# A hybrid S5/SSD layer on one core: strips without an order edge, S5 output blocks among the gate tiles, SSD chain started two tiles later

## The chip, the cores and the metric

The kernel runs on one core of a Trainium2 chip. The metric is the device time of one execution in microseconds (us). It is the median of several runs; the profile comes from one further execution. The core has five engines that work side by side: TensorE (PE, matmuls), VectorE (DVE), ScalarE (ACT), GpSimd (POOL) and SyncE (SP, which here only issues DMAs). Each engine works through its own queue in order.

## The reference

One layer with two parallel branches over 1024 frames of width 1024, in float32, cut to what matters here:

```python
hn   = rmsnorm(h, norm_w)
u_s5, z_s5, z_ssd, xBC, dt_raw = split(hn @ w_in)
y_s5  = s5_branch(u_s5, ...)        # 64 groups of 16 channels, 64 complex states each
y_s5  = y_s5 * sigmoid(y_s5 @ w_glu + b_glu) * silu(z_s5)
y_ssd = gated_group_rmsnorm(ssd(silu(conv(xBC)), dt) + D * x, z_ssd)
h = h + concat(y_s5, y_ssd) @ w_out
h = h + (p @ w_ple) * sigmoid(rmsnorm(h) @ w_gate)
return rmsnorm(h, final_norm_w)
```

The S5 branch is a linear recurrence per channel group, the SSD branch a chunked scan with 16 heads; both are causal in time.

## The kernel before, in words

**Dense tiles.** All large products are "dense tiles": 48 matmuls of 128x128 by 128x512 (8 steps over the contraction, 2 halves of the frames, and 3 products, since each float32 operand is split into a high and a low part, `hi` and `lo`). `wload` (L125 to L135) loads one weight tile on SP, makes `whi` on ACT (L131) and `wlo` on VectorE or, from the 29th tile on, on POOL (L134). The dense tiles in order: 8 tiles for the S5 input `u`; 20 tiles in the order of `SEQ`, 16 conv tiles (`conv_tile`, "c") and 4 gate tiles (`z_tile`, "z"); a second loop with the other 12 gate tiles; 8 GLU tiles; 8 tiles of the first half of the output projection (operand `m`); 8 of its second half (operand `n`, made from the SSD's result); then the gate of the last stage.

**Work between the tiles.** The S5 and SSD branches are Python generators, `s5_chain` and `ssd_chain`. Between (or in the middle of) dense tiles the program calls `pull(gen, n)`, which writes the next `n` steps of the chain into the program. `PU`, `PX`, `PZ`, `PG` and `PO` hold how many steps go beside each tile: `PU` beside the u tiles, `PX` beside the 20 tiles of `SEQ`, `PZ`, `PG`, `PO` for the SSD chain beside the second gate loop, the GLU tiles and the output projection (each twice per tile: in its middle and behind it).

**Who sets the order.** The program is built with `schedule_with_timeline_sim=True`: the builder keeps an estimate of every instruction's time and writes each engine's queue in the order in which instructions become ready by that estimate. Of those that are ready, the one that stands earlier in the program goes first. `in_line` (L191 to L195) adds an order edge without a wait: the second instruction is put into its queue only after the first has been put into its own.

**S5.** `s5_weights` (from L320) works on eight blocks b. For each it loads `br` and `gr`, forms two products (L365, L366) and sums (L368) for `wx`, and forms `CA` from six VectorE operations (L378 to L383). `strips` (L341) then makes a small matrix `Ks` of the block before: 8 matmuls on PE (L345; 16 records), two drains on VectorE (L351, L352) and a store on SP (`Kd`, L353). Each strip matmul has an order edge to the current block's L366. When all blocks are done their memory goes to the next pools. `s5_states` loads `ug` (L396) and makes states (L420), then scans along time on VectorE and ACT. `s5_out` writes eight output blocks: for each, loads of `CAr` (L462), eight of `tp` (L465) and one of `ug`, 16 matmuls (L479, L480), a gelu on ACT (L482) and a store `Yd` (L483). Two blocks' buffers exist at a time; the loads of block b+1 are written ahead of block b's matmuls. After the last block the S5 memory is free; the SSD chain's pool lies in the same place.

**SSD.** `ssd_chain` has a first load step and four steps for each of eight chunks, 33 in all. Step one of a chunk: 16 operations on the decay tile `csB` (L593), its exponential on ACT (L597), score matmuls (L600), products (L602), transposes (L609) and scaled copies `xd` (L613). Step two: loads of the next chunk (`cc` L575, `csB` L578), the output matmuls (L625, L633) and sums (L627, L636, L637). Steps three and four: gate, group norm (L655 to L658), state update (L667, L672) and the store `Sd` (L659). After the chain, `m2raw` (L873) reads the eight `Sd` tiles back through two buffers, ACT scales them (L875) and L218, L219 split them into `nhi` and `nlo`, the operand of the output projection's second half.

**The second gate loop.** It runs over the 12 gate tiles left; behind tile 5 (index 4) and later ones it loads one tile of `m` from `Yd` (L828).

Of the kernel before, what the change touches and what calls it, by code (L numbers as in the profile page):

```python
# [11 lines left out]
ALU = mybir.AluOpType  # L12

P = 128
# [13 lines left out]

PU = [0, 1, 2, 2, 2, 1, 2, 1]
SEQ = "cczzccccccccczzccccc"  # L30
PX = [3, 3, 1, 1, 2, 1, 2, 1, 0, 2, 1, 2, 2, 0, 1, 1, 2, 2, 2, 2]


PZ = [0, 0, 0, 0, 0, 1, 1, 1, 1, 1, 1, 1]
PG = [1, 1, 1, 1, 1, 1, 1, 1]
PO = [1, 1, 1, 0, 0, 0, 0, 0]
NZ = SEQ.count("z")

ZORD = list(range(8, 16)) + list(range(8))
# [16 lines left out]
def hybrid_layer(ctx: ExitStack, tc: tile.TileContext, xT, pT, w_in, w_dt, w_glu, w_out, w_gate, w_ple,  # L56
                 prm, cst, bst, cstt, brow, out):
    nc = tc.nc
    V, S, G, T = nc.vector, nc.scalar, nc.gpsimd, nc.tensor
# [13 lines left out]
    def pr(n, i=None, w=1):  # L73
        a, b = po[n]
        return prm_t[:, a:b] if i is None else prm_t[:, a + i:a + i + w]

    def cs_(n):
        a, b = co[n]
        return cst_t[:, a:b]
# [27 lines left out]
    def psa():  # L107
        return ps_a.tile([P, 512], F32, tag="a", name="psa")
# [33 lines left out]
    def wnext(ahead=1):  # L142
        wfetch(1)
        w = wq.pop(0)
        wfetch(ahead)
        return w
# [43 lines left out]
    def in_line(ins):  # L190

        for a, b in zip(ins, ins[1:]):
            tc.add_manual_dep(b.ins, a.ins.name, mybir.DependencyInfo(mybir.DependencyClass.NoSync, mybir.DependencyReason.DATA),
                              reason="in line")

    def evac(ps, dst, func=AF.Copy):
        for h in range(2):
            S.activation(hf(dst, h), ps[h], func)
# [24 lines left out]
    def pull(gen, n=1):  # L223
        for _ in range(n):
            if next(gen, "end") == "end":
                return False
        return True
# [90 lines left out]
    def s5_weights(Er, Ei, qr, qi, wx):  # L318

        fl = lambda t: t.rearrange("p a b c -> p (a b c)")  # L320
        with ExitStack() as es:
            qb = es.enter_context(tc.tile_pool(name="qb", bufs=1, side="right"))
            Bbd = qb.tile([P, 2, 32, 32], F32, tag="Bbd", name="Bbd")
            G.memset(Bbd, 0.0)
            with tc.tile_pool(name="qt", bufs=1, side="right") as q2:
                bs = q2.tile([P, 2, 32, 16], F32, tag="bs", name="bs")
                dma(bs.rearrange("p a b c -> p (a b c)"), bst)

                bt1 = q2.tile([P, 32, 16], F32, tag="bt1", name="bt1")
                bt2 = q2.tile([P, 32, 16], F32, tag="bt2", name="bt2")  # L330
                for ri, (x, y, op) in enumerate(((qr, qi, ALU.subtract), (qi, qr, ALU.add))):
                    V.tensor_tensor(bt1, bs[:, 0], x[:, :, None].broadcast_to([P, 32, 16]), ALU.mult)
                    V.tensor_tensor(bt2, bs[:, 1], y[:, :, None].broadcast_to([P, 32, 16]), ALU.mult)
                    for g2 in range(2):
                        r = slice(64 * g2, 64 * g2 + 64)
                        V.tensor_tensor(Bbd[r, ri, :, 16 * g2:16 * g2 + 16], bt1[r], bt2[r], op)
                yield
            q2 = es.enter_context(tc.tile_pool(name="q2", bufs=2, side="right"))
            csb = q2.tile([P, 2, 32, 16], F32, tag="csb", name="csb", bufs=1)
            dma(csb.rearrange("p a b c -> p (a b c)"), cstt)  # L340
            def strips(b, CA, behind):  # L341
                kp = psa()
                for q in range(4):
                    for ri in range(2):
                        i_ = T.matmul(kp[32 * q:32 * q + 32, 0:P], Bbd[:, ri, 4 * b + q, :],  # L345
                                      CA[:, ri, q, 0:8, :].rearrange("p a b -> p (a b)"),
                                      start=(ri == 0), stop=(ri == 1), tile_position=(0, 32 * q))
                        in_line((behind, i_))
                Ks = q2.tile([P, 240], F32, tag="Ks", name="Ks", bufs=1)
                G.memset(Ks[:, 0:112], 0.0)  # L350
                V.scalar_tensor_tensor(Ks[:, 112:128], cs_("diag"), pr("s5D", b), kp[:, 0:16], ALU.mult, ALU.add)  # L351
                V.tensor_copy(Ks[:, 128:240], kp[:, 16:P])  # L352
                dma(Kd[b], Ks)  # L353

            for b in range(8):
                br = q2.tile([P, 2, 512], F32, tag="br", name="br", bufs=1)
                gr = q2.tile([P, 2, 512], F32, tag="gr", name="gr")
                w1 = q2.tile([P, 2, 512], F32, tag="w1", name="w1", bufs=1)
                dma(br, brow[:, :, b * 512:(b + 1) * 512].rearrange("r p c -> p r c"))

                src = Gd.rearrange("s (b g) c -> s b (g c)", b=8)[:, b]
                dma(gr.rearrange("p r c -> p (r c)"), src[:, None, :].broadcast_to([8, 16, 1024]))
                wi = wx[:, 8 * b:8 * b + 8]
                g8 = lambda ap: ap.rearrange("p (g c) -> p g c", g=8)
                V.tensor_tensor(wi, br.rearrange("p r (g c) -> p g r c", g=8), g8(gr[:, 0])[:, :, None, :].broadcast_to([P, 8, 2, 64]), ALU.mult)  # L365
                behind = V.tensor_tensor(w1, br, gr[:, 1:2].broadcast_to([P, 2, 512]), ALU.mult)  # L366
                for r, op in ((0, ALU.subtract), (1, ALU.add)):
                    V.tensor_tensor(wi[:, :, r], wi[:, :, r], g8(w1[:, 1 - r]), op)  # L368
                CA = q2.tile([P, 2, 4, 9, 16], F32, tag="CA", name="CA")
                ca1 = q2.tile([P, 4, 9, 16], F32, tag="ca1", name="ca1", bufs=1)  # L370
                ca2 = q2.tile([P, 4, 9, 16], F32, tag="ca2", name="ca2", bufs=1)
                g4 = slice(4 * b, 4 * b + 4)
                sh = [P, 4, 9, 16]
                cr = csb[:, 0, g4, None, :].broadcast_to(sh)
                ci = csb[:, 1, g4, None, :].broadcast_to(sh)
                er = Er[:, J0:J0 + 9, g4].rearrange("p j g -> p g j")[:, :, :, None].broadcast_to(sh)
                ei = Ei[:, J0:J0 + 9, g4].rearrange("p j g -> p g j")[:, :, :, None].broadcast_to(sh)
                V.tensor_tensor(ca1, cr, er, ALU.mult)  # L378
                V.tensor_tensor(ca2, ci, ei, ALU.mult)
                V.tensor_tensor(fl(CA[:, 0]), fl(ca1), fl(ca2), ALU.subtract)  # L380
                V.tensor_tensor(ca1, cr, ei, ALU.mult)
                V.tensor_tensor(ca2, ci, er, ALU.mult)
                V.scalar_tensor_tensor(fl(CA[:, 1]), fl(ca1), -1.0, fl(ca2), ALU.mult, ALU.subtract)  # L383
                for g2 in range(2):
                    dma(CAd[b, g2].rearrange("r n c -> n r c"),
                        CA[64 * g2:64 * g2 + 64].rearrange("p a b c d -> p a (b c d)"))
                if b > 0:
                    strips(b - 1, last, behind)
                last = CA
                yield  # L390
            strips(7, last, behind)
            yield

    def load_u(pool, b):
# [284 lines left out]
    s5 = s5_chain()  # L679
# [110 lines left out]
    def z_tile(m, mid=None):  # L790

        z = pz.tile([P, NT], F32, tag="z", name="z")
        ps = dense(wnext(), xhl, mid=mid)
        if m < 8:
            evac(ps, z, AF.Silu)
        else:
            zk = z.rearrange("p (k t c) -> p t k c", k=8, t=8)
            for h in range(2):
                S.activation(zk[:, 4 * h:4 * h + 4], ps[h].rearrange("p (t k c) -> p t k c", t=4, k=8), AF.Silu)
        dma(Zd[m], z)  # L800
# [4 lines left out]
    with tc.tile_pool(name="p3", bufs=2) as p3:  # L805
        at = {"c": 0, "z": 0}
        for c, n in zip(SEQ, PX):
            m = at[c]
# [3 lines left out]
            else:  # L812
                z_tile(ZORD[m])
            pull(s5, n)
    while pull(s5):
        pass


    es_m = ExitStack()
# [2 lines left out]
    ssd = ssd_chain()  # L822
    for m, n in zip(range(NZ, 16), PZ):
        z_tile(ZORD[m], lambda: pull(ssd, n))

        for i in range(8)[m - NZ - 4:m - NZ - 3] if m >= NZ + 4 else ():
            for h2 in range(2):
                dma(mt[i][64 * h2:64 * h2 + 64].rearrange("p (t c) -> p t c", t=8), Yd[:, :, 2 * i + h2, :])  # L828
        pull(ssd, n)
# [19 lines left out]
    for m in range(8):  # L849
        dma(h_t[m], xT[m])  # L850
        ps = dense(wnext(), mhl, mid=lambda: pull(ssd, PO[m]))
        for h in range(2):
            V.tensor_tensor(hf(h_t[m], h), hf(h_t[m], h), ps[h], ALU.add)
        pull(ssd, PO[m])
    while pull(ssd):
# [46 lines left out]
    for cols in ((slice(0, 384), slice(384, 768)), (slice(768, NT),)):  # L902
        end = cols[-1].stop == NT
        for m in range(8):
            pp = dense(wnext(3), phl, nk=2, cols=cols, bank=psa)
            pg = dense(wnext(3), hhl, cols=cols)
            for i, c in enumerate(cols):
# [3 lines left out]
                last = S.activation(gt, gt, AF.Sigmoid)  # L911
# [129 lines left out]
```

## Time and profile before

| | us |
|---|---|
| median of 3 runs | 1009.69 |
| lowest and highest of them | 1008.46, 1011.22 |
| the profiled execution | 1010.22 |
| its span, first to last instruction | 1008.4 |
| PE busy in the span | 964.2 |
| VectorE busy | 614.2 |
| ACT busy | 462.6 |
| POOL busy | 245.5 |

The profiled execution took 1.8 us more than its span. Matmuls overlap their neighbours in the records, so PE's busy time says when PE had work, not that it was at its peak. The view of waits gives the idle time of an engine with the instruction that ended it. In the views of time, "[6.93 <-DVE CA L383]" behind an instruction says that its engine had stood idle for 6.93 us, until an instruction of VectorE at line 383 that writes CA. PEclk is the granted share of the full TensorE clock.

### The profile page before, as it was taken

Reading aid. Unit: us, or ns where it says so; the run is one execution under the profiler, and the core shown is the slowest. Engines: PE = TensorE matmul, PEld = TensorE weight load, DVE = VectorE, ACT = ScalarE, POOL = GpSimd, SP = SyncE. Lnnn points to the kernel's source line nnn. Section 1 sums busy time; section 2 is a strip of 40 time slices with the busy share of each in tenths; the row PEclk is TensorE's granted clock in tenths of the full one; section 3 lists DMA queues with packets and bytes.
Section 4 is the critical chain, followed back from the end, with each engine's and each line's share of the span. In section 5 each row is a group of like instructions: output and inputs, shape, how many; then the busy total and the mean of one; then the engine's idle time right before and its main releaser. Section 6 shows DMA issues by size and latency. Waiting matters only on the chain. (4 is left out here: it accounts for less than half of the span.)

```text
span 1008.4 us, 13149 instructions
## 1 busy us (share of the span) xinstructions
PE 964.2 (96%) x4992; PEld 809.6 (80%) x4992; DVE 614.2 (61%) x972; ACT 462.6 (46%) x605; POOL 245.5 (24%) x166
## 2 busy tenths in 40 slices
PE   8999979997999999899989999899999999999994
PEld 5778857787888888788778888787888888899994
DVE  7599689953988994000666968679511511444677
ACT  8444122363855544224456754547233522453373
POOL 0000000000000043001134345444332363332353
PEclk9999979998999999999999999999999999999998
DMA  7135778578423136997996868556354330011233
GB/s 296 40 86 142 206 222 270 163 186 208 133 97 105 63 104 192 253 264 210 248 322 175 229 188 230 161 153 188 121 172 145 133 128 21 1 58 53 70 134 115
DMA packets 136270, 158.56 MB, mean 157 GB/s; under 512 B 6288, under 2 KB 108688, under 8 KB 135184
## 3 DMA queue, kind: packets, MB, share of 16 engines
q1 hardware_dynamic: 136208, 157.74, 53.3%
q8 instruction: 39, 0.64, 0.3%
q14 instruction: 23, 0.19, 0.1%
HBM read 118.06 MB, written 39.65 MB: 156 GB/s over the span
## 5 line engine op out<-in xcount | busy, mean ns | idle before, releaser
L134 POOL TENSOR_TENSOR wlo<-wraw,whi 128x1024 fp32r<-128x1024 f32 x52 | 140.2, 2698 | 272.6 <-ACT whi L131 260.5
L131 ACT ACTIVATE whi<-wraw 128x1024 fp32r<-128x1024 f32 x79 | 83.3, 1056 | 241.8 <-PE psd L155 205.2
L155 PE MATMUL psd<-xnlo,whi 128*128 128x512 f32 x592 | 186.2, 394 | 0.2 <-DVE xnlo L766 0.2
L155 PE MATMUL psd<-xnhi,whi 128*128 128x512 f32 x592 | 185.1, 393 | 0.0
L155 PE MATMUL psd<-xnhi,wlo 128*128 128x512 f32 x592 | 184.7, 393 | 0.1
L155 PEld LDWEIGHTS psd<-xnlo,whi 128*128 128x128 f32 x592 | 110.8, 189 | 25.0 <-issue 1.6
L155 PEld LDWEIGHTS psd<-xnhi,wlo 128*128 128x128 f32 x592 | 111.0, 189 | 24.3 <-issue 1.0
L155 PEld LDWEIGHTS psd<-xnhi,whi 128*128 128x128 f32 x592 | 111.0, 189 | 23.1 <-issue 0.4
L593 DVE SCALAR_TENSOR_TENSOR csB<-csB,csM,cst_t 128x128 f32<-128x128 f32 x128 | 45.3, 427 | 101.6 <-DMA m<-Yd 93.5
L566 DVE SCALAR_TENSOR_TENSOR cv<-pad,prm_t,cv 128x1024 f32<-128x1024 f32 x48 | 65.8, 1371 | 11.9 <-ACT cv L564 11.7
L557 POOL MEMSET pad<- 128x3 f32 x16 | 1.6, 104 | 217.1 <-DMA Cd<-pad 186.0
L155 PE MATMUL psd<-hhi,whi 128*128 128x384 f32 (+1 forms) x192 | 50.7, 318 | 0.5 <-DVE gt L910 0.5
L155 PE MATMUL psd<-hlo,whi 128*128 128x384 f32 (+1 forms) x192 | 50.8, 317 | 0.0
L155 PE MATMUL psd<-hhi,wlo 128*128 128x384 f32 (+1 forms) x192 | 50.7, 318 | 0.0
L884 DVE TENSOR_TENSOR h<-h,psd 128x512 f32<-128x512 f32 x16 | 10.4, 683 | 63.3 <-PE psd L155 63.3
L134 DVE TENSOR_TENSOR wlo<-wraw,whi 128x1024 fp32r<-128x1024 f32 x27 | 32.9, 1220 | 15.9 <-ACT whi L131 8.1
L155 PE MATMUL psd<-yhi,whi 128*128 128x512 f32 x128 | 41.0, 398 | 0.0
L155 PE MATMUL psd<-yhi,wlo 128*128 128x512 f32 x128 | 40.7, 395 | 0.0
L155 PE MATMUL psd<-mhi,wlo 128*128 128x512 f32 x128 | 40.1, 391 | 0.0
L155 PE MATMUL psd<-ylo,whi 128*128 128x512 f32 x128 | 40.0, 391 | 0.0
L155 PE MATMUL psd<-mlo,whi 128*128 128x512 f32 x128 | 39.5, 390 | 0.0
L155 PE MATMUL psd<-nhi,wlo 128*128 128x512 f32 x128 | 39.4, 389 | 0.0
(292 smaller groups left out, 1896.1 us busy)
## 6 DMA issues: line engine op xcount, KB each, us to landing
wraw<-in_w_in_dram SPq DMA_DIRECT2D x39, 512.0 KB, 3.8
Cd<-pad SPq DMA_DIRECT2D x16, 512.0 KB, 2.8
Zd<-z SPq DMA_DIRECT2D x16, 512.0 KB, 3.8
ug<-Ud SPq DMA_DIRECT2D x16, 512.0 KB, 6.1
cc<-Cd SPq DMA_DIRECT2D x8, 1024.0 KB, 9.8
csB<-Rd SPq DMA_DIRECT2D x8, 1024.0 KB
wraw<-in_w_out_dram SPq DMA_DIRECT2D x16, 512.0 KB, 5.1
wraw<-in_w_gate_dram SPq DMA_DIRECT2D x16, 512.0 KB, 3.5
```

What stands on the lines that cost most here:

```text
L131: S.activation(hi, raw, AF.Copy)
L134: E.tensor_tensor(lo, raw, f(hi), ALU.subtract)
L155: T.matmul(p, w[:, c], rhs[k][r][:, x], start=(k == 0 and j == 0), stop=(k == nk - 1 and j == 2))
L557: G.memset(pad[:, 8:11, 0:1], 0.0)
L566: conv_last[0] = V.scalar_tensor_tensor(cv, pad[:, d:d + 8, 1:129], pr("convw", 4 * m + d), cv, ALU.mult, ALU.add)
L593: i_ = V.scalar_tensor_tensor(csB[:, h], csB[:, h], csM[:, 16 * k + h:16 * k + h + 1], cap, ALU.subtract, ALU.min)
L884: V.tensor_tensor(hf(h_t[m], h), hf(h_t[m], h), ps[h], ALU.add)
```

## The change

Three things are edited. The strips lose their order edge to L366. `PX` is changed: the first entries from 3, 3, 1 to 1, 4, 2, the last five from 1, 2, 2, 2, 2 to 0, 1, 0, 1, 0; it now holds 24 steps, so that the last five output blocks are left over, and the new list `PS` writes one of them behind each of the first five tiles of the second gate loop, the chain's end behind the fifth. `PZ` starts two tiles later; `PO` goes on for two tiles more, so that the SSD chain has as many pulls as before.

```diff
-PX = [3, 3, 1, 1, 2, 1, 2, 1, 0, 2, 1, 2, 2, 0, 1, 1, 2, 2, 2, 2]
-PZ = [0, 0, 0, 0, 0, 1, 1, 1, 1, 1, 1, 1]
+PX = [1, 4, 2, 1, 2, 1, 2, 1, 0, 2, 1, 2, 2, 0, 1, 0, 1, 0, 1, 0]
+PS = [1, 1, 1, 1, 1]
+PZ = [0, 0, 0, 0, 0, 0, 0, 1, 1, 1, 1, 1]
 PG = [1, 1, 1, 1, 1, 1, 1, 1]
-PO = [1, 1, 1, 0, 0, 0, 0, 0]
+PO = [1, 1, 1, 1, 1, 0, 0, 0]
...
-            def strips(b, CA, behind):
+            def strips(b, CA):
                 kp = psa()
                 for q in range(4):
                     for ri in range(2):
-                        i_ = T.matmul(kp[32 * q:32 * q + 32, 0:P], Bbd[:, ri, 4 * b + q, :],
-                                      CA[:, ri, q, 0:8, :].rearrange("p a b -> p (a b)"),
-                                      start=(ri == 0), stop=(ri == 1), tile_position=(0, 32 * q))
-                        in_line((behind, i_))
+                        T.matmul(kp[32 * q:32 * q + 32, 0:P], Bbd[:, ri, 4 * b + q, :],
+                                 CA[:, ri, q, 0:8, :].rearrange("p a b -> p (a b)"),
+                                 start=(ri == 0), stop=(ri == 1), tile_position=(0, 32 * q))
...
-                behind = V.tensor_tensor(w1, br, gr[:, 1:2].broadcast_to([P, 2, 512]), ALU.mult)
+                V.tensor_tensor(w1, br, gr[:, 1:2].broadcast_to([P, 2, 512]), ALU.mult)
...
-                    strips(b - 1, last, behind)
+                    strips(b - 1, last)
...
-            strips(7, last, behind)
+            strips(7, last)
...
-    while pull(s5):
-        pass
...
     for m, n in zip(range(NZ, 16), PZ):
         z_tile(ZORD[m], lambda: pull(ssd, n))
+        if m - NZ < len(PS):
+            pull(s5, PS[m - NZ])
+        if m - NZ == len(PS) - 1:
+            while pull(s5):
+                pass
```

## Rows read from the trace of the kernel before

**Rows 1.** The page's head: span, and busy time of each engine.

```profile
span 1008.4 us, 13149 instructions
...
PE 964.2 (96%) x4992; PEld 809.6 (80%) x4992; DVE 614.2 (61%) x972; ACT 462.6 (46%) x605; POOL 245.5 (24%) x166
```

**Rows 2.** Waits of PE: releaser, us in total, times, longest.

```profile
PE psa L345 <- DVE CA L383: 6.9, 1, 6.9
PE psa L420 <- DMA ug<-Ud: 5.3, 1, 5.3
PE psa L479 <- DMA tp<-Kd: 4.8, 3, 2.1
PE psa L625 <- DVE xd L613: 3.5, 2, 3.2
...
PE psa L170 <- DVE nl L168: 1.5, 2, 1.1
...
PE psa L625 <- DVE csB L602: 1.4, 1, 1.4
...
PE psa L609 <- DVE st L672: 1.2, 1, 1.2
```

**Rows 3.** PE in order of time, 130 to 160 us: start, us, instruction.

```profile
142.42 1.10 PE L345 MATMUL psa<-CA,Bbd 128*32 128x128 f32 x14 [6.93 <-DVE CA L383]
```

**Rows 4.** Windows behind four waits: us, busy by engine, PEclk, DMA, GB/s.

```profile
142.40:148.40 6.00, 5.98 (x26) 4.58 (x27) 6.00 (x9) 0.00 (x0) 0.00 (x0) 0.53 1.00 277
237.60:244.00 6.40, 6.38 (x31) 6.40 (x32) 2.44 (x2) 2.88 (x4) 0.13 (x2) 0.53 0.51 154
437.60:442.90 5.30, 5.17 (x32) 5.20 (x33) 0.00 (x0) 0.60 (x1) 0.00 (x0) 0.68 1.01 314
522.50:527.50 5.00, 4.94 (x42) 4.37 (x43) 4.86 (x15) 1.86 (x1) 0.18 (x1) 0.66 1.08 367
```

**Rows 5.** VectorE in order of time, S5 weights, blocks 0, 1 and 4.

```profile
108.09 0.76 DVE L383 SCALAR_TENSOR_TENSOR CA<-ca,ca 128x576 f32<-128x576 f32 x1
...
122.42 0.76 DVE L383 SCALAR_TENSOR_TENSOR CA<-ca,ca 128x576 f32<-128x576 f32 x1
124.31 1.23 DVE L365 TENSOR_TENSOR wx<-br,gr 128x1024 f32<-128x1024 f32 x1 [1.14 <-DMA br<-in_brow_dram]
125.46 1.22 DVE L366 TENSOR_TENSOR w<-br,gr 128x1024 f32<-128x1024 f32 x1
...
176.17 0.75 DVE L383 SCALAR_TENSOR_TENSOR CA<-ca,ca 128x576 f32<-128x576 f32 x1
```

**Rows 6.** PE in order of time: the strips of blocks 0 and 4.

```profile
120.02 0.67 PE L345 MATMUL psa<-CA,Bbd 128*32 128x128 f32 x16
...
180.63 0.66 PE L345 MATMUL psa<-CA,Bbd 128*32 128x128 f32 x14
```

**Rows 7.** PE in order of time, 430 to 444 us: the sixth S5 output block.

```profile
437.73 0.46 PE L479 MATMUL psa<-ug,tp 128*128 128x128 f32 x2 [2.08 <-DMA tp<-Kd]
```

**Rows 8.** SP in order of time: third gate tile's store, a load of csB.

```profile
427.96 0.88 SPq L800 DMA_DIRECT2D Zd<-z  x1
...
509.24 0.56 SPq L578 DMA_DIRECT2D csB<-Rd  x1
```

**Rows 9.** VectorE in order of time, 481 to 530 us: around the 3.2 us wait.

```profile
517.94 3.96 DVE L593 SCALAR_TENSOR_TENSOR csB<-csB,csM,cst_t 128x128 f32<-128x128 f32 x11 [2.65 <-DMA csB<-Rd]
521.83 0.68 DVE L613 TENSOR_TENSOR xd<-psa,dt 128x512 f32<-128x512 f32 x1
```

**Rows 10.** SP in order of time: the last chunk's store.

```profile
733.57 0.38 SPq L659 DMA_DIRECT2D Sd<-ys  x1
```

**Rows 11.** ACT in order of time: the last scaled copy of m2raw.

```profile
768.89 1.16 ACT L875 ACTIVATE m<-m2raw,prm_t 128x1024 f32<-128x1024 f32 x1 [2.04 <-DMA m2raw<-Sd]
```

**Rows 12.** PE in order of time: the output projection's second half, steps 0 and 7.

```profile
791.12 0.61 PE L155 MATMUL psd<-nhi,whi 128*128 128x512 f32 x2
...
800.63 0.61 PE L155 MATMUL psd<-nhi,whi 128*128 128x512 f32 x2
```

## The prediction

> **What bounds the kernel now.** I read the page's head first: TensorE (PE) is busy 96% of a span of 1008.4 us [rows 1]. The change neither adds nor removes a matmul, so it can act on three things only: time in which PE stands still, the half-rate time that follows a longer stop, and the end. The view of waits comes next, for PE alone [rows 2]: 6.9 us in one piece at the strips (L345), 5.3 at the S5 states (L420), 4.8 in three pieces at the S5 output blocks (L479), 3.5 and 1.4 at the first SSD chunks (L625), 1.5 and 1.2 where the SSD meets the start of the output projection. The order of time around the longest stop follows [rows 3]: PE stops 6.93 us until L383, the last product that makes the strips' operand CA, is done; dense matmuls stand behind the strip in the queue and wait with it. Then the windows behind four stops [rows 4]. The granted clock is about 0.53 of full speed for 6.0 us after the strips, so 2.8 us are lost, at 1.2 in place of 2.4 GHz; 0.53 for 6.4 us after L420 (3.0 lost); 0.68 for 5.3 us after the longest L479 wait (1.7); 0.66 for 5.0 us after the longer L625 wait (1.7). A stop costs its length and this tail.
>
> The builder orders each engine's queue by its own estimate of times; the chip then keeps that order. A wait on PE is thus a place where another engine is later, against PE, than the builder thought. Program order decides among instructions that are ready, and so decides on PE, where a dense matmul is nearly always ready. It decides little for a step whose data come later than its place.
>
> **Strips.** The 64 edges held each strip's matmuls behind L366 of the next block. Without them a strip goes into PE's queue where the builder sees its operand finished. No work is added and the removed edges are no waits on the chip: the L366 that strip 0 was tied to began at 125.46 [rows 5], the strip itself at 120.02 [rows 6]. Strip 0 now stands near L383 of block 0, which ends at 108.85 [rows 5], and no wait of PE lies thereabouts; I cost it at nothing. Strip 1 comes behind L383 of block 1, which on the chip ends at 123.18. In PE's queue that place is before 120.02 by at least one L365 (1.23 us), and by both products and some of the 1.14 us wait at most (3.6 us), so at 116.4 to 118.8 [rows 5, 6]. PE will wait there 4.4 to 6.8 us. I take 4.7, nearer the short end, since the edge asks only that L366 has been issued, not that it is finished. After it PE runs at half rate; the nearest row is the stop of 5.3 us with 3.0 lost [rows 2, 4]. Together 7.7. PE then arrives at strip 2 later by 7.7, and the 6.93 us there are gone: VectorE's lateness is paid once. The old price is 6.9 + 2.8 = 9.7, so **-2.0 us**. It cannot gain much more: strip 4 runs at 180.63 while its operand is ready at 176.92 [rows 5, 6], so beyond 3.7 us of gain PE would meet VectorE again. At worst the stop at strip 1 takes the whole lateness (6.8 + 3.0) and 3 us more are lost at strip 2: +3. The drains (L351, L352) and the Kd stores come earlier in the VectorE and SP queues, where nothing waits on them soon.
>
> **First entries of PX.** Two S5 state steps move behind the second conv tile, one scan step behind the gate tile after it. None of them ran there: the states wait for memory that the strips release, and only then for their loads [rows 2]. Cost nothing; the 5.3 us at L420 and its tail stay. If that cover were gone, 32 short matmuls would change places with dense ones, which also costs nothing.
>
> **S5 output blocks.** Five of eight are to stand beside the first five gate tiles. But the block meant to follow the third gate tile already runs at 437.73 [rows 7], after that tile's store was issued at 427.96 [rows 8]; the other four stand alike. Data place them, not the program: each block's eight tp loads wait for a buffer that the block two before it frees. The loads keep their turn on SP before weights of the tiles that follow. I take **0**; the three waits (4.8) and the tail (1.7) stay. Bounds: all of it gone (-6.5), or one more late load like the longest (2.1 + 1.7, +3.8).
>
> **SSD chain.** Its pulls begin two gate tiles later, so chunk 0's first matmuls stand after the eighth gate tile of the second loop instead of the sixth. Before, chunk 0 and 1 were later than their places: PE waited 1.4 us at one L625 and 3.2 at another [rows 2]. The second is a jam. VectorE held the next chunk's L593 first in its queue, waiting 2.65 us for csB, and L613, on which PE waited, came only at 521.83 [rows 9]; that csB had been issued at 509.24 [rows 8], 8.7 us before. Every load of the chain moves with it (cc, csB, zc, two E0B, the Sd store), past loads of m on SP. But a load goes out when its buffer is free and SP has nothing earlier in the program, so chunk 0 still loads soon after S5 has ended, while PE asks for it some 20 us later. The two waits and the tail are 1.4 + 3.2 + 1.7 = 6.3. I take **-5.3** and leave 1.0 for new small ones; bounds -6.3 and 0 (they move along). Chunks 3 to 6 keep their places against the GLU tiles one index lower: each still begins behind an odd tile, so those waits stay. At the start of the output projection chunk 6 now stands where the shorter chunk 7 stood: two more L613 of 0.68 us [rows 9] and two state sums of like size, 2.7 us of VectorE, against waits there of 1.5 and 1.2 [rows 2]. I take **+0.8**, between 0 and 2.7. POOL moves along with its parts; it is no releaser in these waits.
>
> **The end of the chain.** Chunk 7's store (L659) went out at 733.57 [rows 10]; the last scaled copy made from it ended at 770.05 [rows 11], 36.5 us later; the second half's first matmul ran at 791.12 and the one that needs the last copy at 800.63 [rows 12]. Less 2.3 us for the two splits, the reserve is 28 us. The chain ends two tiles later; 21 pairs take 9.51 us [rows 12], so a tile of 24 pairs takes 10.9 and the shift is 22, perhaps 26 with the chain's own matmuls between. The reserve holds. **0**.
>
> **Sum.** -2.0 - 5.3 + 0.8 = -6.5 us. The profiled execution took 1010.22 (span 1008.4 and 1.8 around it), 0.5 above the runs' median of 1009.69. So 1003.7 for such an execution, **1003.2** as a median. About 0.3%, 3.0 us, is what a measurement of this kernel can tell from no change: faster means under 1006.7, slower over 1012.7.
>
> **Rivals.** *The waits move along.* The chain's first chunks meet late loads wherever they begin, and the strips only move their stop: -2.0 + 0.8, about 1008.5. For it: the jam is one of queue order, and the builder may set the same order again. Against: the m loads that filled SP are over by then. Chance 0.22.
>
> *The placing does what it says.* The blocks spread out, their loads no longer crowd, and 6.5 us more go: 996.7. Against it stands that the blocks already run behind these tiles [rows 7, 8]. Chance 0.08.
>
> *The tail shows: slower.* Place: the first tile of the output projection's second half, which needs chunk 7. If the chain is later by another tile (10.9 us) than the 26 us counted above, the reserve of 28 is overdrawn by 9, and a stop of that size is followed by some 3 us at half rate [rows 4]: +12, so 1015.2. It decides when chunk 7's store comes less than about 30 us before the second half begins. For it: the loads behind this store take turns through two buffers and cannot be hurried. Against: the last chunk now runs beside tiles that ask little of VectorE. Chance 0.18. The Trainium skill, Perfetto Trace Analysis, Optimization Strategy, says that where regimes have different most-contended engines, performance may be improved by "interleaving those regimes"; by that rule leaving the first seven gate tiles of the second loop without SSD work and heaping it at the end is a loss, and the time would be this rival's. The trace of before bears it out so far only in that the chain's end has 28 us of reserve, not 50.
>
> **How the numbers follow.** The forecast has 0.52. Faster is forecast and second rival, 0.60; same is the first, 0.22; slower the third, 0.18. The range leaves out the third: from 996.5 (second rival) to 1013.5 (the first with the strips at +3 in place of -2).
>
> **What would show it.** Right: the wait at L345 is about 4 to 5 us and stands before 125 us; L420 and L479 keep their waits; no L625 wait over 1.5 us before the GLU; chunk 7's store lies over 30 us before the second half. Wrong: strips that wait in several pieces, L479 waits that are gone, or a PE wait for nhi or nlo.

## The result: slower, and the profile after

| | before | after |
|---|---|---|
| median of 4 runs, us | 1009.08 | 1016.66 |
| lowest and highest, us | 1007.6, 1011.2 | 1015.9, 1018.8 |
| ratio, 95% interval | | 1.0082, 1.0058 to 1.0106 |
| the profiled execution, its span, us | 1010.2, 1008.4 | 1017.1, 1014.9 |

The forecast was 1003.2, in a range from 996.5 to 1013.5. Lines of the changed kernel are one to four higher than before: L345 is now L347, L155 is L157, L479 is L480, L593 is L594, L613 is L614, L625 is L626, L842 is L846, L218 and L219 are L220 and L221, L659 is L660, L875 is L879. The lines of the experiments carry the numbers of their own kernels. First the page's head and PE's view of waits (us in total, times, longest), to be held against [rows 1, 2].

```profile
span 1014.9 us, 13149 instructions
...
PE 963.9 (95%) x4992; PEld 807.2 (80%) x4992; DVE 615.7 (61%) x972; ACT 463.9 (46%) x607; POOL 248.3 (24%) x166
...
PE psa L610 <- ACT zc L656: 6.8, 1, 6.8
PE psa L421 <- DMA ug<-Ud: 5.4, 1, 5.4
PE psa L626 <- issue: 4.7, 2, 4.1
PE psa L480 <- DMA tp<-Kd: 4.1, 2, 2.4
PE psa L172 <- DVE nl L170: 3.8, 2, 2.4
PE psa L347 <- DVE CA L384: 3.3, 3, 2.1
...
PE psd L157 <- DVE nlo L221: 1.9, 2, 1.2
```

PE's work is the same to 0.3 us; only its stops differ. Taken tile by tile, by the start of each dense tile in the two traces, the difference has three parts. Up to the tile that starts at 378 us (382.7 before) it is -4.7 us: the strips gained. From there to the fifth tile of the output projection it is +6.9. In that projection's second half it is +4.5, and then it stays.

**The strips** (PE in order of time): the one stop of 6.93 us [rows 3] has become several.

```profile
123.17 0.66 PE L347 MATMUL psa<-CA,Bbd 128*32 128x128 f32 x14 [2.10 <-DVE CA L384]
...
136.79 0.66 PE L347 MATMUL psa<-CA,Bbd 128*32 128x128 f32 x14 [0.81 <-DVE CA L384]
...
180.51 0.41 PE L347 MATMUL psa<-CA,Bbd 128*32 128x128 f32 x2 [1.09 <-DVE CA L381]
```

**Chunk 0 of the SSD chain** (SP, here with chunk 1's load, VectorE, then PE in order of time).

```profile
484.01 5.13 SPq L579 DMA_DIRECT2D csB<-Rd  x1
...
484.14 4.29 DVE L594 SCALAR_TENSOR_TENSOR csB<-csB,csM,cst_t 128x128 f32<-128x128 f32 x16 [97.38 <-DMA csB<-Rd]
497.01 4.29 DVE L594 SCALAR_TENSOR_TENSOR csB<-csB,csM,cst_t 128x128 f32<-128x128 f32 x16 [8.57 <-DMA csB<-Rd]
501.22 2.48 DVE L603 TENSOR_TENSOR csB<-csB,psa 128x512 f32<-128x512 f32 x4
503.61 0.69 DVE L614 TENSOR_TENSOR xd<-psa,dt 128x512 f32<-128x512 f32 x1
...
504.39 3.38 PE L626 MATMUL psa<-csB,xd 128*64 128x128 f32 x32 [4.12 <-issue]
```

Chunk 0's decay tile is worked on at 484.14. PE asks for its products at 500.27 (504.39 less 4.12), 16 us later. But VectorE's queue holds the sixteen decay operations of chunk 1 in front of chunk 0's products (L603, L614). They wait 8.57 us for chunk 1's load, and PE waits with them. Chunk 0's own data were no reason to wait: ACT had finished its exponential at 491.72 (L598, 489.80 + 1.92), PE its score matmuls and transposes before that, and still L603 ran only at 501.22.

**The start of the output projection** (POOL, VectorE, ACT, then PE in order of time).

```profile
679.24 9.58 POOL L846 TENSOR_TENSOR m<-m,z 128x1024 f32<-128x1024 f32 x1 [3.79 <-DVE m L842]
...
679.09 3.48 DVE L221 TENSOR_TENSOR mlo<-m,mhi 128x1024 fp32r<-128x1024 f32 x3
682.49 0.68 DVE L170 TENSOR_TENSOR nl<-zc,nh 128x512 fp32r<-128x512 f32 x1
683.10 3.48 DVE L221 TENSOR_TENSOR mlo<-m,mhi 128x1024 fp32r<-128x1024 f32 x3
686.50 0.68 DVE L673 TENSOR_TENSOR st<-st,psa 128x512 f32<-128x512 f32 x1
...
688.86 1.06 ACT L220 ACTIVATE mhi<-m 128x1024 fp32r<-128x1024 f32 x1 [5.51 <-POOL m L846]
689.82 1.04 ACT L133 ACTIVATE whi<-wraw 128x1024 fp32r<-128x1024 f32 x1
...
692.17 1.24 ACT L841 ACTIVATE psd<-psd,prm_t 128x512 f32<-128x512 f32 x2
...
694.73 0.69 ACT L656 ACTIVATE zc<-psa,eps_t 128x512 f32<-128x512 f32 x1
...
695.47 1.12 PE L610 MATMUL psa<-cst_t,cc 128*128 128x128 f32 x4 [6.76 <-ACT zc L656]
```

Read it upwards from PE. L610 wants a PSUM bank that the group norm's logarithm (L656) frees. On ACT that logarithm stands behind a split (L220), a weight and two sigmoids, and the split waits for one POOL product, which took 9.58 us. Before, the same product (the seventh of eight) took a quarter of it. The lines of before show two things more: POOL began 0.84 us ahead of VectorE's splits there, and a wait of PE for the same logarithm stood among the GLU tiles (at 637.55), which [rows 2] leaves out (POOL, VectorE, then PE's view of waits).

```profile
687.86 2.41 POOL L842 TENSOR_TENSOR m<-m,z 128x1024 f32<-128x1024 f32 x1 [2.35 <-DVE m L838]
...
688.70 7.14 DVE L219 TENSOR_TENSOR mlo<-m,mhi 128x1024 fp32r<-128x1024 f32 x4 [0.93 <-ACT mhi L218]
...
PE psa L609 <- ACT zc L655: 2.1, 1, 2.1
```

**The second half** (SP, ACT, PE in order of time; [rows 10 to 12] are the same places before).

```profile
754.62 0.36 SPq L660 DMA_DIRECT2D Sd<-ys  x1
...
789.43 1.15 ACT L879 ACTIVATE m<-m2raw,prm_t 128x1024 f32<-128x1024 f32 x1 [1.88 <-DMA m2raw<-Sd]
790.49 1.04 ACT L133 ACTIVATE whi<-wraw 128x1024 fp32r<-128x1024 f32 x1
791.43 6.73 ACT L220 ACTIVATE nhi<-m 128x1024 fp32r<-128x1024 f32 x7
...
793.36 0.61 PE L157 MATMUL psd<-nhi,whi 128*128 128x512 f32 x2
...
795.16 0.74 PE L157 MATMUL psd<-nlo,whi 128*128 128x512 f32 x2 [1.19 <-DVE nlo L221]
803.04 0.73 PE L157 MATMUL psd<-nlo,whi 128*128 128x512 f32 x2 [0.75 <-DVE nlo L221]
...
820.39 0.73 PE L157 MATMUL psd<-nhi,wlo 128*128 128x512 f32 x2 [0.90 <-POOL wlo L136]
```

The eight splits that make `nhi` stand on ACT behind the last scaled copy. Before, they began well ahead of need, each when PE had let go of the old operand. Now they run back to back from 791.43, and PE waits. Of the 4.5 us, 3.3 are lost in the half's first tile, at these two waits and smaller gaps behind them, and 1.2 at 820.39, where PE waits for the low part of a weight from POOL.

**Half rate** (windows: us, busy by engine, PEclk, DMA, GB/s) behind the stops at 412, 504 and 695 us: the granted clock falls as in [rows 4], to the lower of the two levels (0.51 is 1.2 GHz), each time in part while PE still stands.

```profile
410.00:416.00 6.00, 3.90 (x22) 3.94 (x23) 0.00 (x0) 0.65 (x2) 0.00 (x0) 0.72 0.93 274
503.90:507.40 3.50, 3.01 (x30) 3.04 (x32) 3.18 (x8) 0.00 (x0) 0.00 (x0) 0.51 1.17 283
691.60:698.50 6.90, 3.03 (x9) 2.57 (x10) 4.87 (x8) 5.68 (x7) 3.65 (x2) 0.51 0.47 157
```

Between 383 and 740 us PE's stops of over 0.3 us add up to 21.5 us in this trace, against 15.1 before. That sum is used again below.

### The profile page after: what moved, and what is told of

Same layout as the page of the kernel before. It is cut to its first block, busy times and chain, and to the rows that moved or that the text cites. A ratio compares the mean times of both kernels' runs of the same rounds, so it can differ in the third digit from the quotient of the medians.

```text
span 1014.9 us, 13149 instructions
## 1 busy us (share of the span) xinstructions
PE 963.9 (95%) x4992; PEld 807.2 (80%) x4992; DVE 615.7 (61%) x972; ACT 463.9 (46%) x607; POOL 248.3 (24%) x166
## 4 chain that ended last, share of the span: by engine, by line
PE 58%; DVE 15%; DMA 13%; issue 5%; ACT 5%; POOL 2%; SPq 2%; DVEq 0%; ACTq 0%; POOLq 0%
PE psd L157 47%; DMA br<-in_brow_dram 2%; DMA m2raw<-Sd 2%; PE psa L157 2%; DMA csB<-Rd 2%; PE psa L626 2%; DMA Yd<-tp 1%; PE psa L421 1%; DMA tp<-Kd 1%; DVE nlo L221 1%; PE psa L634 1%; DVE csB L594 1%; DVE h L935 1%; PE psa L480 1%; PE psa L481 1%
## 5 line engine op out<-in xcount | busy, mean ns | idle before, releaser
L136 POOL TENSOR_TENSOR wlo<-wraw,whi 128x1024 fp32r<-128x1024 f32 x52 | 137.4, 2644 | 262.0 <-ACT whi L133 236.6
L157 PE MATMUL psd<-xnhi,wlo 128*128 128x512 f32 x592 | 185.1, 392 | 0.2 <-DVE wlo L136 0.2
L157 PE MATMUL psd<-xnlo,whi 128*128 128x512 f32 x592 | 184.7, 392 | 0.0
L157 PE MATMUL psd<-xnhi,whi 128*128 128x512 f32 x592 | 184.0, 392 | 0.0
L157 PEld LDWEIGHTS psd<-xnlo,whi 128*128 128x128 f32 x592 | 110.6, 188 | 24.5 <-issue 1.2
L157 PEld LDWEIGHTS psd<-xnhi,wlo 128*128 128x128 f32 x592 | 110.5, 188 | 24.6 <-issue 1.6
L157 PEld LDWEIGHTS psd<-xnhi,whi 128*128 128x128 f32 x592 | 110.3, 188 | 23.0 <-issue 0.6
L594 DVE SCALAR_TENSOR_TENSOR csB<-csB,csM,cst_t 128x128 f32<-128x128 f32 x128 | 43.2, 411 | 116.9 <-DMA csB<-Rd 116.9
L157 PE MATMUL psd<-hhi,whi 128*128 128x384 f32 (+1 forms) x192 | 50.7, 318 | 0.5 <-DVE gt L914 0.5
L157 PE MATMUL psd<-hlo,whi 128*128 128x384 f32 (+1 forms) x192 | 50.8, 317 | 0.0
L157 PE MATMUL psd<-hhi,wlo 128*128 128x384 f32 (+1 forms) x192 | 50.7, 318 | 0.0
L157 PE MATMUL psd<-nlo,whi 128*128 128x512 f32 x128 | 39.9, 393 | 2.1 <-DVE nlo L221 1.9
L157 PE MATMUL psd<-yhi,whi 128*128 128x512 f32 x128 | 41.1, 397 | 0.0
L157 PE MATMUL psd<-yhi,wlo 128*128 128x512 f32 x128 | 40.7, 394 | 0.0
L157 PE MATMUL psd<-nhi,wlo 128*128 128x512 f32 x128 | 39.6, 390 | 0.9 <-POOL wlo L136 0.9
L157 PE MATMUL psd<-mhi,wlo 128*128 128x512 f32 x128 | 40.4, 394 | 0.0
L157 PE MATMUL psd<-mhi,whi 128*128 128x512 f32 x128 | 40.2, 393 | 0.0
```

Source lines behind the costliest of these rows:

```text
L136: E.tensor_tensor(lo, raw, f(hi), ALU.subtract)
L157: T.matmul(p, w[:, c], rhs[k][r][:, x], start=(k == 0 and j == 0), stop=(k == nk - 1 and j == 2))
L594: i_ = V.scalar_tensor_tensor(csB[:, h], csB[:, h], csM[:, 16 * k + h:16 * k + h + 1], cap, ALU.subtract, ALU.min)
```

## The experiments

Each run is timed beside runs of the kernel before on the same chip, whose median lay between 1005.8 and 1008.3 us there. The expectations were written on the scale of the first runs, where before is 1009. So the ratios are to be compared; the last column is the ratio times 1009.1.

| run | ratio to before (95%) | us on the scale of 1009.1 |
|---|---|---|
| after | 1.0082 (1.0058 to 1.0106) | 1017.4 |
| e1_strips | 1.0026 (1.0010 to 1.0042) | 1011.7 |
| e2_ssd | 1.0061 (1.0040 to 1.0082) | 1015.3 |
| e3_strips_place | 1.0030 (1.0013 to 1.0047) | 1012.1 |
| e4_one_tile | 0.9983 (0.9962 to 1.0004) | 1007.4 |
| e5_order | 0.9977 (0.9955 to 0.9999) | 1006.8 |
| e6_one_tile_order | 0.9898 (0.9864 to 0.9931) | 998.8 |
| e7_before_order | 1.0020 (0.9996 to 1.0045) | 1011.1 |
| e8_pool | 1.0010 (0.9985 to 1.0035) | 1010.1 |
| e9_strips_order | 0.9977 (0.9964 to 0.9989) | 1006.8 |
| e10_strips_place_order | 0.9975 (0.9957 to 0.9992) | 1006.6 |
| e11_tail | 1.0048 (1.0030 to 1.0067) | 1013.9 |
| e12_before_order_sd | 0.9991 (0.9976 to 1.0006) | 1008.2 |
| e13_order_spread | 0.9933 (0.9911 to 0.9956) | 1002.3 |
| e14_one_tile_order_spread | 0.9900 (0.9879 to 0.9920) | 999.0 |
| e15_after_spread | 1.0034 (1.0014 to 1.0054) | 1012.5 |

### The parts alone

e1 is before without the strips' edge:

```diff
-                        in_line((behind, i_))
```

> Only the strips' order edge is taken away; S5 blocks and SSD chain stand as before. The two traces show the conv tiles of the changed kernel running 4.7 us earlier from the third gate tile on. Theory (the strips part is a gain by itself, the loss lies wholly in the SSD part): 1004 to 1005 us, the wait at the strips is cut into several short pieces of 2 us and less, no stretch at half rate near 142 us. Rival (the gain comes with the later S5 states in PX, not with the edge): 1008 to 1010 us.

Both were wrong: 1011.7, a loss. The strips did gain: at 380 us the tiles ran 7.0 us ahead of before. All of it was gone by 536 us, in two places. At the first group norm (L169, at 503.34) PE stood for 3.31 us, where before it stood for 0.59; that is 2.7 of the 7.0. The rest went at chunk 1 (PE's view of waits, then VectorE and PE in order of time):

```profile
PE psa L169 <- ACT nh L167: 3.3, 1, 3.3
...
513.05 0.35 DVE L592 SCALAR_TENSOR_TENSOR csB<-csB,csM,cst_t 128x128 f32<-128x128 f32 x1 [7.62 <-DMA csB<-Rd]
...
525.18 0.68 DVE L612 TENSOR_TENSOR xd<-psa,dt 128x512 f32<-128x512 f32 x1
...
525.91 1.97 PE L624 MATMUL psa<-csB,xd 128*64 128x128 f32 x16 [6.24 <-DVE xd L612]
```

The second is the jam of [rows 9], one chunk's decay operations ahead of the other's products, and larger. What in the builder's estimate set this order was not tried.

e2 is before with only the SSD lists changed:

```diff
-PZ = [0, 0, 0, 0, 0, 1, 1, 1, 1, 1, 1, 1]
-PO = [1, 1, 1, 0, 0, 0, 0, 0]
+PZ = [0, 0, 0, 0, 0, 0, 0, 1, 1, 1, 1, 1]
+PO = [1, 1, 1, 1, 1, 0, 0, 0]
```

> Only PZ and PO are changed: the SSD chain begins two tiles later, the strips keep their edge and the S5 blocks stand as before. Theory (the SSD shift alone makes the loss): 6.9 us more between the gate tiles and the output projection and 4.5 us more at its second half, so about 1020 us. Rival (the S5 blocks beside the gate tiles crowd the start of the chain, and the shift without them costs only the 4.5 us at the end): about 1013 us.

1015.3, between the two: the shift alone makes most of the loss. Its trace has the stop at L609 (5.17 us) and the waits at the second half, as after.

e3 is the changed kernel with the two SSD lists of before.

> The changed kernel with PZ and PO of the kernel before: strips without the edge, five S5 blocks beside the first five gate tiles, the SSD chain at its old place. Theory (the SSD shift alone makes the loss): 1004 to 1005 us, the second half of the output projection waits no longer than before, chunk 7's store is some 57 us ahead of it. Rival (the S5 blocks beside the gate tiles cost by themselves, since their loads now share the queue with the chain's first loads): 1008 us or more.

1012.1, over the rival's bound, but the reading attached to it fails: e1, without the blocks, is as slow (1.0026 and 1.0030). So all that is changed in `PX`, the S5 blocks among it, costs nothing. The second half waits for nothing here, and chunk 7's store lies 57.8 us ahead of it.

e4 is the changed kernel with the chain one tile later in place of two:

```diff
-PZ = [0, 0, 0, 0, 0, 0, 0, 1, 1, 1, 1, 1]
-PO = [1, 1, 1, 1, 1, 0, 0, 0]
+PZ = [0, 0, 0, 0, 0, 0, 1, 1, 1, 1, 1, 1]
+PO = [1, 1, 1, 1, 0, 0, 0, 0]
```

> The changed kernel with the SSD chain one tile later than before in place of two. Theory (a reserve is overdrawn at the end): the last tile's worth of lateness costs what the second half loses, so here the 4.5 us at the second half are gone, the reserve ahead of it being about 48 us between chunk 7's store and the first matmul. The 6.9 us ahead of it depend on which chunk meets the start of the output projection, so 1005 to 1012 us. Rival (the cost grows by the tile): half of the loss of two tiles, about 1010.5 us, with waits for nhi and nlo half as long.

1007.4: the theory. The store comes 48.8 us ahead, and no wait for `nhi` or `nlo` is left. One tile is better than none by 0.5% and better than two by 1%, so the cost does not grow with the shift.

### VectorE's order

The edge added (lines are cut; `held` collects the products of a chunk):

```diff
                     if k == 0:
                         in_line((conv_last[0], i_))
+                    for d in held:
+                        in_line((d, i_))
+                held = []
...
-                    V.tensor_tensor(csB[:, 4 * g:4 * g + 4], ...
+                    held.append(V.tensor_tensor(csB[:, 4 * g:4 * g + 4], ...
...
-                            V.tensor_tensor(dst[:, 8 * i:8 * i + 8], xv, ...
+                            held.append(V.tensor_tensor(dst[:, 8 * i:8 * i + 8], xv, ...
```

> The changed kernel with one order edge more on VectorE: the decay operations of a chunk (on csB) are put into its queue only behind the products (csB and xd) of the chunk before. Theory (the stop of 4.1 us at chunk 0 is VectorE's queue: the next chunk's decay operations stood ahead of the products PE waits for, and waited 8.6 us for their load): that stop and its tail at half rate, 5.8 us together, are gone, so 1010 to 1012 us, with the 6.8 us stop and the waits for nhi and nlo left. Rival (the load itself is what limits the chunk): the stop stays, moved by one chunk, 1016 to 1017 us.

> The kernel with the SSD chain one tile later (strips and S5 blocks as changed), with the same order edge. It had stops of 2.2 us at L626 (chunk 0) and 4.1 us at L610 with 1.7 at half rate behind each. Theory (queue order): the second goes, since it stood behind a decay operation that waited for its load; 1000 to 1003 us. Rival (the load limits): 1005 us as without the edge.

> The kernel before with the same order edge and nothing else. Theory (queue order): the 3.2 us stop at L625 and its tail of 1.7 go, about 5 us less than before. Rival (the load limits): within 1 us of before.

On the changed kernel (e5) the edge is worth 10.6 us, more than expected, since the stop at L610 fell to 1.2 us as well. With one tile's shift (e6) it is worth 8.6, and that kernel is 1.0% faster than before; PE's stops in the stretch of the sum above are down to 8.4 us. On the kernel before (e7) it is worth nothing, against the theory. The stop at L625 is gone, but 3.40 us appear at L651, which waits for a PSUM bank. The bank is freed by a sum on VectorE, and that waits for chunk 0's store. Its product was ready at 509.1 (507.90 + 1.23), but SP stood at another store (SP, VectorE, PE in order of time):

```profile
505.78 7.26 SPq L803 DMA_DIRECT2D Zd<-z  x1
513.14 0.38 SPq L130 DMA_DIRECT2D wraw<-in_w_in_dram  x1
513.61 0.94 SPq L662 DMA_DIRECT2D Sd<-ys  x1
...
521.29 1.12 DVE L630 SCALAR_TENSOR_TENSOR ys<-cc,prm_t,psa 128x128 f32<-128x128 f32 x4 [1.87 <-DMA Sd<-ys]
...
522.56 1.09 PE L651 MATMUL psa<-cst_t,cc 128*128 128x128 f32 x4 [3.40 <-DVE ys L630]
```

e12 takes that store off SP's queue:

```diff
-                dma(Sd[k].rearrange("a p c -> p a c"), ysb)
+                nc.scalar.dma_start(out=Sd[k].rearrange("a p c -> p a c"), in_=ysb)
```

> The kernel before with the order edge, and with the stores of the chunks (Sd) issued by ACT in place of SP. With the edge alone the 3.2 us stop at L625 was replaced by one of 3.4 us at the transposes of B, which waited for a PSUM bank, that for a sum on VectorE, and that for chunk 0's store, which SP issued 4.5 us after the product was ready, behind a gate tile's store. Theory (a queue's order again, SP's): this stop and its half-rate stretch of 6.8 us go, 1003 to 1006 us. Rival (DMA is full there and the store lands late anyway): within 2 us of the kernel with the edge alone, near 1011 us.

1008.2, between the two: the stop at L651 is 2.16 us, and behind it the clock is at 0.50 for 3.3 us, where with the edge alone it was at 0.60 for 6.8. SP's order was part of it; what makes the rest was not tried.

### Strips, with the order mended

> The kernel before with the strips' edge taken away and the order edge on VectorE added. Strips alone were 7 us ahead at the end of the gate tiles and lost it at a stop of 6.2 us at chunk 1, with 5 us more at half rate. Theory (that stop is VectorE's order: the decay operations of chunk 2 ahead of chunk 1's products): the stop is gone, 998 to 1003 us. Rival (DMA is full from 470 to 510 us whatever the order, so PE meets the late loads in another place): 1006 to 1010 us.

> The same with the S5 blocks beside the first five gate tiles as well; it is the changed kernel with the SSD chain at its old place and the order edge. Theory (placing the S5 blocks is worth nothing): within 2 us of the run without the placing. Rival (their loads beside the chain's cost): over 3 us slower than that run.

e9 gives 1006.8, 4.3 us under e7, so about what the strips gained in the trace; of e9's two expectations it is the rival's time. The stop at chunk 1 is gone, as the theory has it, but the 3.4 us at the first group norm stay, as in e1 (3.3). e10, with the S5 blocks placed as well, is the same (0.9975). The placing is worth nothing with either order.

### POOL and the tail

e8 moves one product:

```diff
-        E = G if m < 7 else V
+        E = G if m < 6 else V
```

> The changed kernel with the last but one of the eight m products with z on VectorE in place of POOL (the one that took 9.6 us beside VectorE's splits, where others take 2.4). Theory (this one POOL operation makes the 6.8 us stop, since the split behind it holds ACT's queue and with it the group norm whose PSUM bank PE needs): the stop falls under 2 us and half of the half-rate stretch goes, so 1007 to 1011 us. Rival (chunk 6's group norm is late there by its own chain): the stop stays over 4 us, 1014 to 1017 us.

1010.1, 7.3 us less than the changed kernel, and no stop at L610 at all: the theory.

e11 makes `nhi` on VectorE:

```diff
-            S.activation(hi, src[m], AF.Copy)
+            (V.tensor_copy(hi, src[m]) if nm == "n" else S.activation(hi, src[m], AF.Copy))
```

> The changed kernel with the eight copies that make nhi on VectorE in place of ACT. Theory (the 4.5 us lost at the second half of the output projection are the eight splits, which stand on ACT behind the eight scaled copies): the waits for nlo go, the step n0 to n3 loses under 1.5 us, so 1012 to 1014 us. Rival (the loads of m2raw set the time): the waits stay at 3 us or more in all, 1015 to 1018 us.

1013.9, and no wait for `nhi` or `nlo` is left in the trace: the theory.

### The crowd of loads

Here each pair of `m` loads is held on SP behind the store of the gate tile before (`stored` lists these stores):

```diff
-                dma(mt[i][64 * h2:64 * h2 + 64]...
+                in_line((stored[-2], dma(mt[i][64 * h2:64 * h2 + 64]...
```

> The changed kernel with VectorE's order edge, and each pair of m loads held behind the store of the gate tile before it, so that they go out one pair per tile in place of all sixteen from 464 to 500 us. Theory (the loads crowd: a weight tile issued behind eight m loads landed 7 us later, ACT waited for it and the first group norm stood behind): the 4.3 us wait at the group norm and its 1.7 at half rate are gone, 998 to 1001 us. Rival (the weight waits for its buffer, not for the queue): 1004 to 1006 us.

> The fastest kernel so far (SSD chain one tile later, order edge) with the m loads spread in the same way. Theory (crowding): the wait of 2.2 us at chunk 0 and its 1.7 at half rate go, 992 to 995 us. Rival (chunk 0's wait is the length of its own chain of exponential and products): 996 to 998 us.

> The changed kernel, only with the m loads spread; no order edge. Theory (crowding made chunk 1's decay tile late, so VectorE's order alone would not have hurt): the stop of 4.1 us at chunk 0 falls under 2 us, 1009 to 1013 us, the stop of 6.8 us at the start of the output projection staying. Rival (order alone): the stop at chunk 0 stays over 3 us, 1014 to 1018 us.

In e5 the 4.26 us at the first group norm (L171) end with ACT, and ACT had waited for a weight tile that SP issued behind eight `m` loads (two other loads stand between the fourth and the fifth) and a store (SP, ACT, PE in order of time):

```profile
494.25 5.00 SPq L835 DMA_DIRECT2D m<-Yd  x4
499.34 1.07 SPq L804 DMA_DIRECT2D Zd<-z  x1
500.52 0.69 SPq L132 DMA_DIRECT2D wraw<-in_w_in_dram  x1
...
507.89 1.06 ACT L133 ACTIVATE whi<-wraw 128x1024 fp32r<-128x1024 f32 x1 [5.75 <-DMA wraw<-in_w_in_dram]
...
511.70 0.65 ACT L169 ACTIVATE nh<-zc 128x512 fp32r<-128x512 f32 x1
...
512.40 0.50 PE L171 MATMUL psa<-nh,ones_r 128*128 128x512 f32 x1 [4.26 <-ACT nh L169]
```

With the loads spread (e13) that stop is gone: 1002.3, 4.5 us less than e5, a time between the two expectations. e14 shows the limit: 999.0, the same as e6, and chunk 0's wait keeps its 2.25 us to the hundredth. So it is not the crowd; the rival's reading, chunk 0's own chain, is the one left. e15, without any order edge, takes 4.9 us less than the changed kernel: the stop at chunk 0 falls to 1.89 us and has no half-rate time behind it. VectorE's queue has the same order there and waits as long for chunk 1's load (8.53 us). But that wait ends 8.7 us earlier (chunk 1's decay operations begin at 488.33 in place of 497.01), and PE asks for chunk 0 only 6.4 us earlier (493.83 in place of 500.27), so 2.2 us less of it reach PE. The stop at L610 stays (5.1). So two things make the jam: an order that puts a later chunk's operations first, and the lateness of the load that they wait for. Mending the order takes the stop away (e5). What an earlier load takes is less sure: in e8 and e11, whose edits leave this place as it is, the stop is 4.6 and 3.2 us, so of e15's 2.2 us about half may be chance.

## Why the prediction was wrong

**SSD chain, -5.3: the step that failed.** It said that PE would ask for chunk 0 some 20 us after the loads, and that the waits would go. PE did ask 16 us after the decay tile's arrival, and still waited 4.1 us; with 1.7 us lost at half rate behind it that is 5.8, against the 6.3 of before, so 0.5 of the forecast 5.3 came. The step took the jam for lateness of the chunk that PE wants, which margin cures. It was an order in VectorE's queue, in front of another chunk's late load; I had read that off [rows 9], and yet priced the shift as if the builder would not write such an order again. The rival of the waits that move along named this rightly. With the order fixed by an edge, one tile later is worth 7.8 us (e6 against e10), two tiles nothing (e5 against e10). e13 and e11 point to what the second tile costs: the crowd of loads at the first group norm (4.5 us), which e6 does not meet, and the tail (3.5 us, tried without the edge).

**Start of the output projection, +0.8 within 0 to 2.7: outside the bounds.** The stop was 6.8 us where waits of 1.1 (at 696.50) and 1.2 (at 703.91) had been; the other 0.5 of the 1.5 in [rows 2] stood at 630.71, among the GLU tiles, where the prediction did not place it. The sentence that failed is "POOL moves along with its parts; it is no releaser in these waits". POOL's product took 2.41 us there. The bounds held VectorE's extra work and no longer POOL operation. e8 shows that this product makes the whole stop. VectorE's extra work did show, just ahead of it: PE waited 2.45 us at 683.23 for `nl` (L170), which stood behind three splits, and in e8 that wait is still there (2.62).

**End of the chain, 0: failed.** The shift of the store was forecast as 22 to 26 us; it ate 18.8 of the 57.5 us between store and second half. The mistake is the reserve. I held the last scaled copy against the second half's last step and added one pair of splits, 2.3 us. But all eight splits stand behind that copy on ACT. The first began 36.8 us after the store (791.43 less 754.62), and the second half begins 38.7 after it. Waits appeared with the store 38.7, 38.8 and 39.4 us ahead (after, e5, e8) and not at 46.0 and 48.8 (e6, e4), so the need lies between 39.4 and 46.0 while ACT makes the splits, and not at 29.5. The third rival was right in place and sign. But its price, 12 us, and its condition, a store less than about 30 us ahead, were both off. The place it named, the half's first tile, cost 3.3, and 1.2 more followed; with the splits on VectorE (e11) neither is left. That the total came near its 1015.2 is luck: the two steps above make up the rest.

**Strips, -2.0: right in sign, mis-sized.** 4.5 us of waits in five pieces, none with half-rate time behind it, where I had one stop of 4.7 and 3.0 more; by the tiles -4.7, of which 1.2 stood already ahead of the strips. PE came to strip 1 at 121.07 (123.17 less 2.10), not between 116.4 and 118.8, so it waited less than half of the 4.7; why it came later stays open. "Strips that wait in several pieces" was named as a sign against the forecast. What the step did not count is that such a gain meets the chain's first chunks: e1 gives it all back, and e9, with VectorE's order mended, is 4.3 us under e7.

**Right:** nothing from the first entries of `PX` (e1 and e3 differ in all of `PX` and take the same time); the wait at L421 stays (5.4). **S5 output blocks, 0:** L480 waits 4.1 us against 4.8, and two pairs of runs (e1 and e3, e9 and e10) show no difference.

## What to carry to other kernels

A wait in an in-order queue need not be cured by starting earlier or later: find which instruction stands in front, and fix the order with an edge, or its load, before moving work around it. When a chain is moved, price what its operations will run beside in the new place, on every engine, and count a reserve to the last operation queued behind the late one, not to the late one itself. A gain far upstream counts only after it has passed the next tight place; here that took an order edge, after which one tile's shift made the fastest kernel (e6, 1.0% under before; e14 is level with it).

## What was not expected of the hardware

One POOL product took 9.58 us in place of 2.41, and 9.60 and 9.58 in e2 and e11. It began 0.15 us after VectorE had started six splits and one more product, each with both inputs in SBUF; these ended at 686.58, 7.34 us into it, and 9.58 less 7.34 leaves 2.24, nearly the usual time. That fits a product that stood still until VectorE was through. In the kernel before and in e5 POOL began first, by 0.84 and 0.86 us; its product took 2.41 in both, and it was VectorE that lost: four splits took 7.14 and 7.13 us, where the six of the changed kernel take 3.48 for each three. A second case of that kind: VectorE's L641, 1.23 us alone, took 3.40 beside a POOL product of 2.40:

```profile
669.24 2.40 POOL L136 TENSOR_TENSOR wlo<-wraw,whi 128x1024 fp32r<-128x1024 f32 x1
...
669.31 3.40 DVE L641 TENSOR_TENSOR ys<-ys,zc 128x1024 f32<-128x1024 f32 x1 [1.41 <-POOL ys L638]
```

The Trainium skill, SBUF — State Buffer, "Who interferes with whom", says that a VectorE instruction with two SBUF inputs contends with a GpSimd instruction that reads SBUF. The Trainium skill, SBUF — State Buffer, "SBUF: two separate sides", adds that the one that starts first has the shared ports for the whole instruction, and that the other is blocked. The rows agree in both directions (9.58 in place of 2.41, 3.40 in place of 1.23), and suggest one thing more: the 9.58 us leave POOL no turn between VectorE's seven instructions in a row.
